# Down-projection of token blocks 0 and 1 as seven block products, with the up-projection's partial sums held in PSUM

## The chip, the core and the metric

The program runs on one core of one Trainium2 chip. TensorE (PE) multiplies, with PEld as its weight loads; VectorE (DVE), ScalarE (ACT) and GpSimd (POOL) do the element-wise work; SyncE (SP) issues most DMAs. The metric is the device time of one execution in microseconds, the median of several runs.

## The reference, cut to what matters

One layer: a combined input projection, chunk-band attention and an mLSTM (together "the mixers"), an output projection, and a feed-forward network with a short convolution. All sums are in float32. The change touches the feed-forward network:

```python
def conv_ffn(h, buf, w_up, w_conv, b_conv, w_down):
    S = h.shape[1]
    u = h @ w_up                                  # 1024 -> 2 * 2816
    ext = jnp.concatenate([buf.astype(u.dtype), u], axis=1)
    y = b_conv
    for j in range(CONV_W):                       # width 3, causal
        y = y + ext[:, j:j + S] * w_conv[j]
    gate, up = jnp.split(y, 2, axis=-1)
    out = (jax.nn.gelu(gate, approximate=True) * up) @ w_down   # 2816 -> 1024
    return out, ext[:, S:]
```

and in the layer: `x = x + rms_norm(conv_ffn(rms_norm(x)))`. There are 2048 prompt tokens (16 tiles of 128) and 8 x 16 sample tokens (one tile).

## The kernel before

Every float32 operand of a matmul is split into a high part (a cast to fp32r, by ACT) and a low part (the rest, by DVE); `mm3` (lines 93 to 97) makes three matmuls of a product: high x high, high x low, low x high. The helper `split` (1264 to 1266) does the two steps for an operand in SBUF, so most splits stand under lines 1265 and 1266 in the profile.

The program has these stages, in order of time:

- **Mixers** (to about 1050 us): 28 weight groups of the input projection (two halves of the tokens, 14 groups each; loop at line 1201). Steps of attention and mLSTM, kept in two pipes, are laid between the projection's steps by `pump` according to planned PE and DVE costs.
- **Output projection** (about 1050 to 1313 us), `project`, which stores the rows x2 in DRAM (`x2d`). `h2_units` prepares the first block's normed, transposed operands.
- **Feed-forward**, three token blocks (`FBLOCKS`: six tiles, six tiles, five tiles), each an up stage and a down stage.

The **up stage** runs over 22 column tiles f of 128 (`NF`), each giving a gate and an up row of 768 tokens. It already uses Winograd's form of Strassen's scheme: seven products P1 to P7 of 4 x 3 matmuls (384 wide, 320 in block 2) in place of eight (`product`, line 1411). The seven token-side operands `B[i]` are made by `h2_units`; the weight-side sums are made in block 0 by four DVE operations per f (`load_quads`, line 1282) and kept in DRAM (`wsd`) for blocks 1 and 2. The products' partial sums x1, x2, x3 are formed in SBUF: one ACT copy (1489) and DVE additions out of PSUM (1491, 1493, 1419, 1508). `conv` then applies the convolution (ACT at 1438, two DVE operations at 1439 and 1440, ACT's gelu at 1442), DVE multiplies gate and up (1514), and the result goes to DRAM (`gd`, 768 values a partition per f).

The **down stage** multiplies that by `w_down` in the plain way: for each half of the output columns `dh`, for each of 22 k, for each of six token tiles one `mm3` of 512 columns (`down`, 1547). The six accumulators are two PSUM banks of tag "mm" and two double banks of tag "big". The operand `gr` is fetched again for each dh and split (`split_g`, 1465) into `gh`, `gl`, held in four buffers of tag "w3", so two k at a time. Weights come four 512-column pieces at a time (`load_down`, 1311) into one of two buffer pairs `wh`, `wl`. Raw fetches land in buffers of tag "q" (`quad`, 512 columns, 11 of them) and "yq" (`row`, 1024 columns, 4 of them). Between the k, `ahead.step()` lays in the next block's `h2_units` and the residual rows of the block before (`later`, 1369: two fetches, a DVE step, a POOL addition, a DMA from POOL's queue).

The tile layer decides the order of the instructions of each engine from the program order, priorities and buffers that come free; it inserts all waits. `keep_in_program_order` pins a DMA's place. Each DMA on SP's queue waits for the one issued eight before it.

## Time and profile before

| | us |
|---|---|
| median of 3 runs (lowest, highest) | 2795.22 (2794.82, 2800.33) |
| span of the profiled execution, first to last instruction | 2784.7 |
| PE busy, DVE busy, ACT busy in that span | 2723.8, 1876.3, 1409.1 |

The page gives a span and no total of the profiled execution; the runs' median is 10.5 us above the span, for what lies before the first and after the last instruction. "Busy" of an engine is the time in which at least one of its instructions ran. Matmuls overlap in the pipeline, so the mean duration of one (about 0.39 us for 512 columns) is longer than the distance between two; what a matmul costs is read as a stretch of time without idle PE divided by the number of matmuls in it. In a table of stretches a row gives the stretch and its length, then busy time and count of PE, PEld, DVE, ACT and POOL, the granted TensorE clock, the DMA engines' busy share and GB/s. In a list of waits a row gives who waited for whom, the total, how often, and the longest. In a list of groups a row ends with the group's busy time and the mean of one in ns, then the engine's idle time before it and who ended it.

### The profile page before, as it was taken

The page shows a single profiled execution, that of the slowest core. Times are in us where ns is not written, and L with a number is a line of the kernel's source. Part 1 is how long each engine was busy: PE and PEld are TensorE (multiplying, and loading weights), DVE is VectorE, ACT ScalarE, POOL GpSimd, SP SyncE. Part 2 cuts the span into 40 slices and gives each one's busy share as a digit, 9 for nine tenths or more (in the row PEclk, how much of TensorE's full clock was granted, in tenths as well). Part 3 has the DMA queues.
Part 4 walks back from the last instruction along what each step waited for, and adds up shares of the span by engine and source line. Part 5 has one row for each costly group of instructions (what it writes and reads, how often), then busy time and mean ns, then how long its engine had stood idle before and what let it go on. Part 6 is the DMA issues. An engine that isn't in the chain of part 4 may idle for free.

```text
span 2784.7 us, 47088 instructions
## 1 busy us (share of the span) xinstructions
PE 2723.8 (98%) x16587; PEld 2548.3 (92%) x16587; DVE 1876.3 (67%) x3447; ACT 1409.1 (51%) x2836; POOL 437.4 (16%) x895
## 2 busy tenths in 40 slices
PE   8999999999999999999999999999999999999998
PEld 7899999998899998888999988899999878999887
DVE  5344455656556668666999986457877864888855
ACT  4355555644356666544454555345455543555543
POOL 1000010212000003244111110011111310222220
PEclk9999999999999999999999999999999999999999
DMA  5544355557555555356655455644544774555585
GB/s 185 155 119 136 103 174 162 164 157 217 162 173 148 144 179 171 107 176 227 187 172 167 167 176 174 219 142 153 160 152 141 276 263 152 172 179 180 192 309 190
DMA packets 311883, 486.05 MB, mean 175 GB/s; under 512 B 55426, under 2 KB 150622, under 8 KB 311518
## 3 DMA queue, kind: packets, MB, share of 16 engines
q1 hardware_dynamic: 271134, 442.92, 50.1%
q10 hardware_dynamic: 38592, 33.83, 3.6%
q0 software_dynamic: 1920, 6.29, 0.6%
q8 instruction: 130, 2.13, 0.3%
q14 instruction: 107, 0.88, 0.1%
HBM read 359.36 MB, written 126.70 MB: 175 GB/s over the span
## 4 chain that ended last, share of the span: by engine, by line
PE 55%; DVE 2%; DMA 1%; issue 1%; ACT 1%; POOL 1%; SPq 0%; DVEq 0%; POOLq 0%; ACTq 0%
PE uec L95 6%; PE uec L96 6%; PE uec L97 6%; PE dn L97 4%; PE dn L96 4%; PE dn L95 4%; PE ua L97 3%; PE ua L95 3%; PE ua L96 3%; PE dnm L97 2%; PE dnm L95 2%; PE dnm L96 2%; PE wo L97 2%; PE wo L95 2%; PE wo L96 2%; PE ub L96 1%
## 5 line engine op out<-in xcount | busy, mean ns | idle before, releaser
L95 PE MATMUL uec<-B,wuh 128*128 128x384 f32 (+1 forms) x720 | 234.9, 328 | 2.2 <-DVE uu L1419 1.1
L96 PE MATMUL uec<-B,wuh 128*128 128x384 f32 (+1 forms) x720 | 235.1, 327 | 0.0
L97 PE MATMUL uec<-B,wul 128*128 128x384 f32 (+1 forms) x720 | 233.9, 327 | 0.0
L1266 DVE TENSOR_TENSOR gl<-gr,gh 128x768 fp32r<-128x768 f32 (+3 forms) x141 | 120.4, 863 | 145.8 <-ACT gh L1265 144.5
L1265 ACT CAST gh<-gr 128x768 fp32r<-128x768 f32 (+3 forms) x141 | 102.0, 735 | 200.1 <-PE dn L96 183.2
L1265 ACT CAST wuh<-wu 128x512 fp32r<-128x512 f32 x255 | 141.7, 617 | 112.1 <-PE uec L96 103.2
L95 PE MATMUL dn<-wdh,gh 128*128 128x512 f32 x466 | 182.4, 391 | 2.3 <-DVE ug L1419 2.3
L96 PE MATMUL dn<-wdl,gh 128*128 128x512 f32 x466 | 183.4, 394 | 0.0
L97 PE MATMUL dn<-wdh,gl 128*128 128x512 f32 x466 | 167.9, 396 | 0.0
L1266 DVE TENSOR_TENSOR wul<-wu,wuh 128x512 fp32r<-128x512 f32 x255 | 164.6, 683 | 2.8 <-DMA x2d<-mx 2.8
L393 DVE CUSTOM_DVE_ANT_0 tmp<-s,nb 128x640 f32<-128x640 f32 (+4 forms) x128 | 94.4, 737 | 96.6 <-PE s L383 94.8
L95 PE MATMUL vo<-wi_h,hT 128*128 128x256 f32 x544 | 155.1, 285 | 0.6 <-DVE mt L199 0.6
L97 PE MATMUL vo<-wi_h,hT 128*128 128x256 f32 x544 | 155.6, 286 | 0.0
L96 PE MATMUL vo<-wi_l,hT 128*128 128x256 f32 x544 | 154.8, 285 | 0.0
L95 PEld LDWEIGHTS uec<-B,wuh 128*128 128x128 f32 x720 | 135.0, 188 | 4.2 <-DVE uu L1419 1.6
L95 PE MATMUL qk<-hT,wi_h 128*128 128x384 f32 (+1 forms) x384 | 128.7, 335 | 7.4 <-ACT qk_st L224 6.6
L96 PEld LDWEIGHTS uec<-B,wuh 128*128 128x128 f32 x720 | 135.2, 188 | 0.2
L97 PEld LDWEIGHTS uec<-B,wul 128*128 128x128 f32 x720 | 135.1, 188 | 0.0
L406 DVE TENSOR_TENSOR ptl<-pt,pth 128x640 fp32r<-128x640 f32 (+4 forms) x128 | 93.6, 737 | 57.1 <-ACT pth L405 56.0
L394 ACT ACTIVATE tmp<-tmp,mn 128x640 f32<-128x640 f32 (+4 forms) x128 | 97.6, 762 | 64.6 <-DVE mn L393 61.9
L96 PE MATMUL qb<-hT,wi_h 128*128 128x384 f32 (+1 forms) x384 | 127.8, 333 | 0.0
L96 PE MATMUL qk<-hT,wi_h 128*128 128x384 f32 (+1 forms) x384 | 127.6, 332 | 0.0
(412 smaller groups left out, 8873.0 us busy)
## 6 DMA issues: line engine op xcount, KB each, us to landing
wu<-in_w_up SPq DMA_DIRECT2D x220, 256.0 KB, 4.1
wu<-wsd SPq DMA_DIRECT2D x176, 256.0 KB, 4.2
wdr<-in_w_down SPq DMA_DIRECT2D x132, 256.0 KB, 5.6
gr<-gd SPq DMA_DIRECT2D x78, 384.0 KB, 3.6
wi_raw<-in_w_in SPq DMA_DIRECT2D x52, 512.0 KB, 4.0
wsd<-ws SPq DMA_DIRECT2D x88, 256.0 KB, 2.8
gd<-g SPq DMA_DIRECT2D x44, 384.0 KB, 3.5
kraw<-kTd SPq DMA_DIRECT2D x112, 128.0 KB, 3.2
```

What stands on the lines that cost most here:

```text
L95: nc.tensor.matmul(out, ah, bh, start=start, stop=False, skip_group_check=onto)
L96: nc.tensor.matmul(out, ah, bl, start=False, stop=False, skip_group_check=onto)
L97: nc.tensor.matmul(out, al, bh, start=False, stop=stop, skip_group_check=onto)
L393: nc.vector.tensor_tensor_reduce(o_, s_, b_, 1.0, 3e38, ALU.add, ALU.min, accum_out=mn)
L394: nc.scalar.activation(tmp[:, :n], tmp[:, :n], AF.Exp, bias=mn, scale=-1.0, accum_out=rsum[:, i % 4, hh:hh + 1])
L406: nc.vector.tensor_tensor(s.ptl[:, sl, qc], ptv, s.pth[:, sl, qc], op=ALU.subtract)
L1265: nc.scalar.copy(h, r)
L1266: nc.vector.tensor_tensor(l, r, h, op=ALU.subtract)
```

## The change

It has five parts.

1. **Seven products in the down stage of blocks 0 and 1** (`FAST`). The activations are cut in four (k below or above 11, first or second three token tiles: A11, A12, A21, A22), the weights likewise (k, output half: B11, B12, B21, B22). `SEQUENCE` names the seven products; each is 11 k x 3 token tiles x `mm3` with 512 columns, and they go alternately into two sets of three PSUM accumulators; every second product of set 0 adds onto what stands there. `leave` copies or adds the sets out after each product. Block 2 keeps the plain form.
2. **The weight differences** T1 to T4 are made once, in the mixers: `folds` fetches w_down in 22 pieces of 512 KB, makes four DVE subtractions of 256 columns on each and stores it to DRAM (`wtd`). A piece is fetched every 12 steps, combined 9 steps and stored 14 steps after its fetch.
3. **The activation sums** S1 to S4 are made in the up stage (`store_a`), four DVE operations of 384 columns for each pair (f, f + 11), in place; they and A11, A12, A22 are stored in DRAM (`ad`) as pieces of 384 columns, seven a pair. f therefore runs in the order 0, 11, 1, 12, ... (`FORDER`).
4. **The up stage's sums in PSUM** in all blocks: P1's result is copied by ACT into bank d, P6 adds onto it, ACT copies d into bank c, P5 and P3 add onto c, P4 adds onto d, P2 onto a. P7 is copied out by ACT. DVE is left with two additions of the up row; the gate row is copied out by ACT. P1 of the next f stands ahead of P4 and P3 of this one. Two pairs of matmuls named "mark" write the double banks once, ahead of block 0.
5. **Buffers**: 12 "q" (11 before), 6 "yq" (4), two `drs` (1); the SBUF scratch of the software DMA queue is set to 4096 bytes a partition; `h2_units` of blocks 1 and 2 is spread over more steps.

```diff
+NK = NF // 2
+FAST = (0, 1)
+FOLD_STEPS = 12
+FORDER = [f for k in range(NK) for f in (k, k + NK)]
...
+            if not late:
+                yield 0.0, 0.0
...
-            for i in range(6):
+            for i in range(6 if late else 8):
...
+    def folds():
...
+        def load(i):
+            k, c = pieces[i]
+            live[i] = v4(pr.tile([P, D], F32, tag="fold", name=f"fold{k}_{c}", bufs=3))
+            tc.keep_in_program_order(nc.sync.dma_start(live[i], v4(I["w_down"][k])[:, :, c * 256:(c + 1) * 256]))
+
+        def combine(i):
+            a, b, c, d = [live[i][:, x] for x in range(4)]
+            for o, x, y in ((a, b, a), (b, c, b), (c, c, a), (d, d, c)):
+                nc.vector.tensor_tensor(o, x, y, op=ALU.subtract)
+
+        def store(i):
+            k, c = pieces[i]
+            tc.keep_in_program_order(nc.sync.dma_start(v4(wtd[k])[:, :, c * 256:(c + 1) * 256], live.pop(i)))
+
+        for n in range(FOLD_STEPS * (len(pieces) + 2)):
+            for lag, do in ((0, load), (9, combine), (14, store)):
+                i, r = divmod(n - lag, FOLD_STEPS)
+                if r == 0 and 0 <= i < len(pieces):
+                    do(i)
+            yield
...
+            if 2 <= gi <= 12:
+                next(fold, None)
...
+    SEQUENCE = [("A11", B11, 0, False), ("A12", B21, 1, False), ("S2", T2, 0, True), ("S4", B22, 1, False),
+                ("S3", T3, 0, True), ("S1", T1, 1, False), ("A22", T4, 0, True)]
...
+        def first(f):
+            a, dc = ps_mm(f"ua{b}_{f}"), ps_big(f"udc{b}_{f}")
+            product(P1, W.pop((P1, f)), a)
+            nc.scalar.copy(dc[:, :n], a[:, :n])
+            return a, dc[:, 0:512], dc[:, 512:1024]
...
-            product(P1, w[0], a)
-            nc.scalar.copy(x1[:, :n], a[:, :n])
-            product(P6, w[1], d_)
-            nc.vector.tensor_tensor(x2[:, :n], x1[:, :n], d_[:, :n], op=ALU.add)
-            product(P7, w[2], e)
-            nc.vector.tensor_tensor(x3[:, :n], x2[:, :n], e[:, :n], op=ALU.add)
-            product(P5, w[3], c)
-            second(uu, x3, c)
...
-            product(P2, w[0], a, onto=True)
-            nc.scalar.copy(ug[:, 2:2 + n], a[:, :n])
-            product(P4, w[1], e, onto=True)
-            nc.vector.tensor_tensor(uu[:, 2:2 + n], x2[:, :n], e[:, :n], op=ALU.add)
-            product(P3, w[2], c, onto=True)
-            second(ug, x2, c)
...
+            product(P6, W.pop((P6, f)), d_, onto=True)
+            nc.scalar.copy(c[:, :n], d_[:, :n])
+            product(P7, W.pop((P7, f)), e)
+            nc.scalar.copy(p7[:, :n], e[:, :n])
+            product(P2, W.pop((P2, f)), a, onto=True)
             nc.scalar.copy(ug[:, 2:2 + n], a[:, :n])
...
+            product(P5, W.pop((P5, f)), c, onto=True)
+            for o, x, y in halves(uu, p7, c):
+                nc.vector.tensor_tensor(o, x, y, op=ALU.add)
...
+                nxt = first(FORDER[fi + 1])
+            product(P4, W.pop((P4, f)), d_, onto=True)
+            nc.vector.tensor_tensor(uu[:, 2:2 + n], p7[:, :n], d_[:, :n], op=ALU.add)
             yu = conv(uu, 1, f)
+            product(P3, W.pop((P3, f)), c, onto=True)
+            for o, _, y in halves(ug, None, c):
+                nc.scalar.copy(o, y)
...
+            def leave(p):
+                acc = sets[SEQUENCE[p][2]]
+                if p in (0, 2, 4, 6):
+                    kept[p] = trio(f"x{p}_")
+                for j in range(3):
+                    if p in (0, 2, 4):
+                        nc.scalar.copy(kept[p][j], acc[j])
+                    elif p == 1:
+                        nc.vector.tensor_tensor(kept[0][j], kept[0][j], acc[j], op=ALU.add)
+                        close(j, 0, kept[0][j])
...
+                    for k in range(4 * c, min(4 * c + 4, NK)):
+                        i = 6 * p + k // 2
+                        if k % 2 == 0:
+                            if i >= 1:
+                                split_a(i + 1)
+                                fetch_a(i + 4)
...
+                        for j in range(3):
+                            tt = slice(k % 2 * 384 + j * P, k % 2 * 384 + (j + 1) * P)
+                            mm3(sets[set_][j], ah[:, tt], al[:, tt], wh[:, wk], wl[:, wk],
+                                start=not onto and k == 0, stop=k == NK - 1, onto=onto)
+                        steps += 1
+                        if steps % 2 == 0:
+                            ahead.step()
+                leave(p)
...
-    nc = bacc.Bacc("TRN2", target_bir_lowering=False, num_devices=1)
+    nc = bacc.Bacc("TRN2", target_bir_lowering=False, num_devices=1, dynamic_dma_scratch_size=4096)
```

In `SEQUENCE` a row is the activation operand, the weight block, the accumulator set and whether the product adds onto what the set holds. `split_a` and `fetch_a` are the activations' `split_g` and `fetch`: one call handles two k of 384 columns, so 768 columns as before, in the same four "w3" buffers; `down_rows` takes the place of the loop in `load_down`, with four 512-column pieces a chunk as before.

## The prediction

> **What bounds the kernel now.** First the page's head and busy times, then a table of eight stretches: the mixers (0 to 1050 us), the output projection (to 1313), and up and down stage of blocks 0, 1 and 2.

> ```profile
> span 2784.7 us, 47088 instructions
> PE 2723.8 (98%) x16587; PEld 2548.3 (92%) x16587; DVE 1876.3 (67%) x3447; ACT 1409.1 (51%) x2836; POOL 437.4 (16%) x895
> ```

> ```profile
> 0.00:1050.00 1050.00, 1014.18 (x7314) 986.44 (x7315) 576.59 (x1410) 547.93 (x1305) 96.91 (x291) 1.00 0.53 159
> 1050.00:1313.00 263.00, 258.01 (x1390) 216.44 (x1389) 186.66 (x290) 126.88 (x302) 96.97 (x130) 1.00 0.49 161
> 1313.00:1642.00 329.00, 322.46 (x1828) 318.80 (x1827) 303.55 (x459) 168.71 (x268) 61.98 (x89) 0.99 0.54 178
> 1642.00:1836.00 194.00, 192.77 (x863) 157.26 (x863) 109.27 (x150) 93.59 (x157) 6.47 (x21) 1.00 0.55 181
> 1836.00:2155.00 319.00, 318.47 (x1828) 318.06 (x1826) 247.04 (x367) 163.96 (x272) 42.99 (x96) 1.00 0.48 154
> 2155.00:2348.00 193.00, 192.39 (x860) 156.00 (x861) 123.70 (x163) 90.63 (x153) 36.99 (x46) 1.00 0.68 230
> 2348.00:2620.00 272.00, 272.00 (x1851) 271.43 (x1850) 235.84 (x480) 155.19 (x274) 64.43 (x182) 1.00 0.56 178
> ```

> PE is idle 1.2 and 0.6 us in the two down stages, 6.5 us in the up stage of block 0, 0.5 in that of block 1, none in that of block 2, at a granted clock of 0.99 to 1.00. So matmuls taken out of a down stage shorten it directly, as long as what feeds PE keeps up. What holds PE up from 1330 us on is this list of waits:

> ```profile
> PE ua L97 <- DVE wul L1266: 3.0, 2, 1.6
> PE dn L95 <- DVE ug L1419: 2.3, 3, 1.4
> PE dnm L95 <- ACT gh L1265: 2.1, 3, 1.5
> PE uec L95 <- DVE uu L1419: 1.1, 1, 1.1
> ```

> with five smaller ones of 3.0 us together: operands that arrive late, none of them for long.

> **What a matmul costs.** Two stretches without idle PE, the first with 512-column matmuls alone, the second with 384-column ones alone:

> ```profile
> 1760.00:1820.00 60.00, 60.00 (x262) 49.02 (x261) 21.84 (x28) 19.23 (x29) 0.00 (x0) 1.00 0.55 180
> 1900.00:2100.00 200.00, 200.00 (x1149) 200.00 (x1148) 156.22 (x231) 101.45 (x164) 25.17 (x55) 1.00 0.47 151
> ```

> 60/262 = 0.229 us and 200/1149 = 0.174 us.

> **Part 1, seven products.** A block's down stage has 22 k x 6 tiles x 2 halves x 3 = 792 matmuls of 512 columns; seven products have 7 x 11 x 3 x 3 = 693. Gone are 198 in two blocks: 198 x 0.229 = 45.3 us. The form of a matmul is the same, and each product's accumulators rest during the product after it (99 x 0.229 = 22.7 us), so no copy out of PSUM should stop PE. The four "mark" matmuls cost 4 x 0.174 = 0.7 us.

> What feeds PE gets more to do in less time (170 us in place of 193). An operand pair of 768 columns still serves 18 matmuls, 4.1 us, but for the same 18 matmuls there are two weight pieces to split in place of one. Rows for it:

> ```profile
> L1266 DVE TENSOR_TENSOR wdl<-wdr,wdh 128x512 fp32r<-128x512 f32 x88 | 58.3, 715 | 9.8 <-ACT wdh L1265 9.8
> L1266 DVE TENSOR_TENSOR gl<-gr,gh 128x768 fp32r<-128x768 f32 x77 | 77.8, 1010 | 107.8 <-ACT gh L1265 107.5
> L1265 ACT CAST wdh<-wdr 128x512 fp32r<-128x512 f32 x88 | 49.3, 617 | 13.9 <-DMA wdr<-in_w_down 7.9 <-PE uec L96 5.9
> L1265 ACT CAST gh<-gr 128x768 fp32r<-128x768 f32 x77 | 64.2, 833 | 132.9 <-PE dn L96 127.6 <-DMA wdr<-in_w_down 3.3 <-DVE f L1376 1.5
> L1340 DVE COPY fr<-dn 128x512 f32<-128x512 f32 x12 | 7.4, 680 | 1.0 <-PE dn L97 1.0
> L1110 ACT COPY b<-h2T_pt 128x512 f32<-128x512 f32 x20 | 11.4, 582 | 3.4 <-PE h2T_pt L1093 2.9 <-PE dn L96 0.5
> ```

> A block has 77 weight pieces (44 before) and 38.5 operand pairs (44). DVE: +33 x 0.715 - 5.5 x 1.010 = +18.0 us; its 12 copies out become 12 additions of about the same 0.68. In block 1: 123.7 + 18.0 = 141.7 of 170 us, 83% (64% before); block 0: 75%. ACT in block 1: 90.6 + 33 x 0.617 - 5.5 x 0.833 + 12 x 0.582 = 113 us, 67%. The row to compare with is the up stage of block 0: DVE is busy 303.6 of 329 us (92%) there and PE idle for 2.0%. So DVE costs between 0 and 2% of 341 us, 6.8. Of the waits at the stages' seams, up to 3 us may go, since the first product needs only one double bank. I take +3 us, bounds -3 to +7.

> The pieces' sizes, from the list of DMA issues (the last column is us from issue to landing):

> ```profile
> wdr<-in_w_down SPq DMA_DIRECT2D x132, 256.0 KB, 5.6
> gr<-gd SPq DMA_DIRECT2D x78, 384.0 KB, 3.6
> ```

> DMA in block 1: 230 GB/s x 193 us = 44.4 MB, + 33 x 0.262 - 5.5 x 0.393 = 50.9 MB, over 170 us 299 GB/s, and the share goes from 0.68 to 0.88. It is uneven even now:

> ```profile
> 2180.00:2200.00 20.00, 20.00 (x96) 16.32 (x95) 19.38 (x23) 12.04 (x19) 9.37 (x10) 1.00 0.96 337
> 2260.00:2280.00 20.00, 20.00 (x89) 16.32 (x88) 10.92 (x15) 10.97 (x21) 1.85 (x6) 1.00 1.01 360
> ```

> The engines were full in both, DVE 97% busy in the first, and PE lost nothing: prefetch carried it. Block 0 comes to 41.6 MB, 244 GB/s. I take no cost; the price without that cover is a rival below.

> **Part 2, weight differences in the mixers.** 22 x 4 DVE subtractions of 256 columns, and 22 fetches and 22 stores of 512 KB. The nearest rows, a 256-column split, and PE's wait for a late fetch in the mixers:

> ```profile
> L356 DVE TENSOR_TENSOR vhl<-vraw,vhl 128x256 fp32r<-128x256 f32 x40 | 16.9, 423 | 18.5 <-ACT vhl L355 18.3
> PE cus L781 <- DMA cs<-in_state_c: 5.0, 6, 2.0
> ```

> 88 x 0.423 = 37 us, against 1050 - 577 = 473 us in which DVE is idle; 23 MB of DMA on 159 x 1050 = 167 MB, a share of 0.60 after 0.53. PE is idle 36 us in the mixers. What is late if this cover fails: a store on SP's queue that waits for its subtraction, or a fetch that waits for a buffer, holds the fetches of attention and mLSTM behind it. A store stands 14 steps behind its fetch. A re-laid order may also save waits. Bounds: -5 (that wait gone) to 22 x 5.0/6 = 18 us. I take +3, 36 us growing like the DMA load (14%, 5 us) being nearer the low end than the high one.

> **Parts 3 and 4, the up stage.** DVE loses three additions of 384 columns per f and gets four subtractions per pair; ACT gets three copies per f more:

> ```profile
> L1493 DVE TENSOR_TENSOR x<-x,uec 128x384 f32<-128x384 f32 x42 | 23.1, 550 | 11.3 <-PE uec L97 11.2
> L1489 ACT COPY x<-ua 128x384 f32<-128x384 f32 x42 | 20.1, 478 | 32.8 <-PE ua L97 32.7
> L1442 ACT ACTIVATE y<-y 128x768 f32<-128x768 f32 x44 | 37.3, 847 | 72.5 <-DVE y L1440 72.5
> ```

> DVE: -3 x 0.55 + 2 x 0.55 = -0.55 us per f in blocks 0 and 1, of about 14.6 us; ACT: +3 x 0.478 = +1.4 us, from 164/319 = 51% to 61% in block 1. New is that PE waits for ACT twice in a chain: P1, copy, P6, copy, P5. In the built program's order 24 to 26 matmuls stand between P6 and P5 of one f (4.2 us) to cover a copy of 0.48. I take 0; low end -6 (the up stages' late operands, 3.0 + 1.1 and smaller ones, vanish); the high end is the third rival. The pieces stored (7 of 192 KB a pair in place of 2 of 384 KB) meet a DMA share of 0.48 to 0.54.

> **Part 5.** Two more bounds by reading: the buffers only relax waits. A smaller scratch may make POOL wait for its previous DMA; nothing that PE needs soon stands behind it but the norm factors of the next block. 0, at most a few us.

> **The sum.** 2784.7 - 45.3 + 0.7 + 3 + 3 + 0 = 2746.1 us of span; the runs' median lies 2795.2 - 2784.7 = 10.5 above it: **2756.6 us**, 1.4% faster. The likeliest case alone: low ends used by half (-8) to -3 + 18 + 7 above, say 2745 to 2778.

> **Rivals.**

> 1. *The mixers' queue is held.* Each of the 22 stores costs PE 0.83 us, the high bound of part 2: 2756.6 - 3 + 18 = 2772. For it: SP issues in order, and PE's waits on DMA exist there. Against: PE's waits from DMAs are few, and the store comes long after its operand. Chance 0.12.
> 2. *The down stage of block 1 becomes DMA-bound.* The extra 6.5 MB fall where the engines are full, at 354 GB/s: +18 us, 2772. For it: the two rows at 0.96 and 1.01. Smaller transfers are slower too: the mixers' 0.53 at 159 GB/s means 300 at a full share, 338 in this stage (230/0.68); at 300 the stage's 50.9 MB take 170 us, exactly its length. Against: those rows show PE not waiting. Chance 0.10. [...]
> 3. *Slower: ACT's copies come late in the up stage.* ACT works in order, and the copy of d into c stands right behind a gelu that waits for the convolution on DVE. Row:

> ```profile
> ACT y L1442 <- DVE y L1440: 93.7, 46, 5.1
> ```

> At its longest, 5.1 + 0.85 + 0.48 = 6.4 us against 4.2 of cover, PE stands 2.25 us; in each of the 44 f of blocks 0 and 1 that is 99 us: 2856. It decides from 0.88 us per f, (2795.2 - 2756.6)/44. For it: DVE is 92% busy in block 0, so its queue is long. Against: the mean of that wait is 93.7/46 = 2.0 us, and it starts before P6 does. Chance 0.09.
> 4. *No gain:* the splits, not PE, set the down stage's pace, and it keeps its 193 us. 2756.6 + 45.3 - 3 = 2799. For it: two weight pieces and an operand pair per 4.1 us through one ACT and one DVE. Against: 83% is below the 92% at which PE lost 2%. Chance 0.05.

> **How the numbers follow.** The forecast has the other 0.64. A difference of 0.2% (5.6 us) is about what a measurement of this kernel can tell from none. Faster: 0.64 + 0.12 + 0.10, less 0.02 for a mild form of rival 3 beside them: 0.84. Same: rival 4 and that mild form, 0.06. Slower: 0.10. The range 2745 to 2788 takes in rivals 1 and 2 and their sum, and leaves out 3 and 4 and little below.

> **What would show it.** Right: 198 fewer 512-column matmuls, stages of about 171 us between the first and last of them in blocks 0 and 1, PE idle below 5 us in each; the output projection starting within 20 us of where it did. Rival 1: longer waits of PE on DMAs before 1050 us. Rival 2: waits of ACT or DVE on wdr or ar fetches in the second down stage, and a share near 1. Rival 3: waits of P5, P6 or P3 on ACT or DVE in every f, and an up stage of block 0 over 340 us. Wrong altogether: PE idle over 45 us more than now.

## The result, and the profile after

The changed kernel takes 2809.85 us (median of 5 runs, 2809.18 to 2815.61); the kernel before, run beside it, 2798.94 (2794.82 to 2800.33). The ratio is 1.0053, with a 95% interval of 1.0038 to 1.0068: slower by 0.5%, where 1.4% faster was forecast. First the head of the page of the profile after, then the table of stretches, cut where the same stages begin in this kernel (mixers and output projection as one, up and down stage of blocks 0, 1 and 2, the tail).

```profile
span 2808.1 us, 47256 instructions
PE 2705.9 (96%) x16393; PEld 2529.3 (90%) x16393; DVE 1888.4 (67%) x3443; ACT 1518.6 (54%) x3164; POOL 451.9 (16%) x895
```

```profile
0.00:1347.00 1347.00, 1286.09 (x8707) 1212.57 (x8708) 788.73 (x1785) 672.55 (x1606) 190.95 (x421) 0.99 0.57 172
1347.00:1691.00 344.00, 328.46 (x1828) 323.40 (x1827) 292.69 (x431) 193.30 (x333) 61.78 (x85) 0.98 0.58 188
1691.00:1865.00 174.00, 170.62 (x766) 138.90 (x765) 129.91 (x190) 112.31 (x201) 18.36 (x30) 1.00 0.72 240
1865.00:2183.00 318.00, 318.00 (x1825) 317.91 (x1824) 236.29 (x338) 188.30 (x333) 42.40 (x90) 1.00 0.57 176
2183.00:2369.00 186.00, 176.22 (x767) 141.04 (x766) 139.46 (x201) 109.92 (x201) 41.67 (x53) 0.97 0.80 272
2369.00:2640.00 271.00, 270.22 (x1839) 269.37 (x1838) 206.45 (x367) 179.97 (x380) 66.19 (x176) 1.00 0.59 181
2640.00:2801.00 161.00, 156.23 (x671) 126.09 (x670) 92.62 (x131) 61.60 (x110) 29.74 (x39) 0.99 0.72 250
```

Against the eight stretches of before: up to block 0's up stage 1313 became 1347 us (+34), that up stage 329 became 344 (+15), down stage 0 194 became 174 (-20), up stage 1 319 became 318 (-1), down stage 1 193 became 186 (-7), up stage 2 272 became 271 (-1), and the rest 165 became 168 (+3). Together +23, the difference of the spans (2808.1 - 2784.7 = 23.4). Part of it is no loss: the profile of before shows a quick execution, as e5 below tells. The matmuls did go: 16587 to 16393 is 194 fewer, 198 less the four marks. So the gain of the down stages is there, in part, and the mixers and up stage 0 ate it.

By kind, PE's idle time rose from 60.9 (2784.7 - 2723.8) to 102.2 us (2808.1 - 2705.9), +41.3. But PE's busy time fell by 17.9 only, not by the 44.6 that the removed matmuls were worth. The mean granted clock says why: 0.998 of full speed before, 0.990 after, so 0.002 x 2784.7 = 5.6 us lost before and 0.010 x 2808.1 = 28 us after. These 22 us are matmuls at half speed; -44.6 + 41.3 + 22 = 18.7 of the 23.4 (the other 5 stay unassigned). The table of stretches of the kernel after, around one stall in up stage 0, shows such a loss:

```profile
1562.61:1566.02 3.41, 3.41 (x21) 3.41 (x21) 2.80 (x5) 1.54 (x2) 0.00 (x0) 1.00 0.54 190
1566.02:1569.44 3.42, 0.76 (x5) 0.44 (x3) 1.38 (x2) 2.55 (x5) 0.00 (x0) 1.00 0.83 159
1569.44:1572.85 3.41, 2.31 (x7) 2.31 (x8) 3.41 (x7) 0.72 (x2) 1.22 (x2) 0.50 0.65 216
1572.85:1576.26 3.41, 3.41 (x12) 3.41 (x12) 2.45 (x5) 1.07 (x2) 1.14 (x2) 0.50 0.61 190
1576.26:1579.68 3.42, 3.42 (x21) 3.42 (x20) 3.11 (x5) 1.64 (x3) 0.49 (x1) 1.00 0.22 83
```

PE stands for 2.66 of 3.42 us. Then the clock is 0.50 for two such windows, and a window without a gap holds 12 matmuls in place of 21. This stall cost its own length and then half of two windows. Of the 13 stretches at a clock of 0.50 in this profile (the end of the program left out) 11 last one window of 3.41 us and two last two.

### The profile page after: what moved, and what is told of

Same layout as the page of the kernel before. It is cut to its first block, busy times and chain, and to the rows that moved or that the text cites. A ratio compares the mean times of both kernels' runs of the same rounds, so it can differ in the third digit from the quotient of the medians.

```text
span 2808.1 us, 47256 instructions
## 1 busy us (share of the span) xinstructions
PE 2705.9 (96%) x16393; PEld 2529.3 (90%) x16393; DVE 1888.4 (67%) x3443; ACT 1518.6 (54%) x3164; POOL 451.9 (16%) x895
## 4 chain that ended last, share of the span: by engine, by line
PE 68%; DMA 14%; DVE 9%; issue 4%; ACT 3%; POOL 1%; SPq 1%; DVEq 0%; ACTq 0%; POOLq 0%
PE udc L101 5%; PE udc L102 5%; PE udc L103 5%; PE dn L103 3%; PE dn L102 3%; PE dn L101 3%; PE ua L102 3%; PE ua L101 3%; PE ua L103 2%; DMA wu<-in_w_up 2%; PE dnm L103 2%; PE pt L73 2%; PE dnm L102 2%; PE dnm L101 2%; PE qb L101 2%
## 5 line engine op out<-in xcount | busy, mean ns | idle before, releaser
L101 PE MATMUL udc<-B,wuh 128*128 128x384 f32 (+1 forms) x720 | 236.6, 329 | 7.0 <-DVE uu L1641 7.0
L102 PE MATMUL udc<-B,wuh 128*128 128x384 f32 (+1 forms) x720 | 235.9, 328 | 0.0
L103 PE MATMUL udc<-B,wul 128*128 128x384 f32 (+1 forms) x720 | 235.6, 328 | 0.0
L101 PEld LDWEIGHTS udc<-B,wuh 128*128 128x128 f32 x720 | 135.9, 189 | 9.1 <-DVE uu L1641 8.9
L1310 DVE TENSOR_TENSOR wdl<-wdr,wdh 128x512 fp32r<-128x512 f32 x198 | 129.1, 699 | 18.6 <-ACT wdh L1309 18.4
L102 PEld LDWEIGHTS udc<-B,wuh 128*128 128x128 f32 x720 | 135.8, 189 | 0.2
L103 PEld LDWEIGHTS udc<-B,wul 128*128 128x128 f32 x720 | 135.7, 189 | 0.0
L1309 ACT CAST wdh<-wdr 128x512 fp32r<-128x512 f32 x198 | 112.7, 617 | 34.9 <-DMA wdr<-in_w_down 10.7
L102 PE MATMUL dn<-wdl,ah 128*128 128x512 f32 x308 | 123.4, 401 | 5.7 <-DVE wdl L1310 5.7
L103 PE MATMUL qk<-hT,wi_l 128*128 128x384 f32 (+1 forms) x384 | 128.0, 333 | 0.0
L103 PE MATMUL qb<-hT,wi_l 128*128 128x384 f32 (+1 forms) x384 | 127.2, 331 | 0.0
## 6 DMA issues: line engine op xcount, KB each, us to landing
wu<-in_w_up SPq DMA_DIRECT2D x220, 256.0 KB, 3.8
wu<-wsd SPq DMA_DIRECT2D x176, 256.0 KB, 4.0
wdr<-in_w_down SPq DMA_DIRECT2D x110, 256.0 KB, 5.3
wsd<-ws SPq DMA_DIRECT2D x88, 256.0 KB, 2.8
wdr<-wtd SPq DMA_DIRECT2D x88, 256.0 KB, 6.3
ar<-ad_S SPq DMA_DIRECT2D x40, 384.0 KB, 4.7
```

Of the source, the lines that this page charges most:

```text
L101: nc.tensor.matmul(out, ah, bh, start=start, stop=False, skip_group_check=onto)
L102: nc.tensor.matmul(out, ah, bl, start=False, stop=False, skip_group_check=onto)
L103: nc.tensor.matmul(out, al, bh, start=False, stop=stop, skip_group_check=onto)
L1309: nc.scalar.copy(h, r)
L1310: nc.vector.tensor_tensor(l, r, h, op=ALU.subtract)
```

## The experiments

Eighteen kernels ran, each against the kernel before on the same chip. Times are medians; the ratio to before has its 95% interval. Beside these runs the kernel before took medians of 2789.36 to 2794.64 us, by the chip, so a time is read through its ratio. "Block 0 starts" is the beginning of its up stage: 1313.5 us in the profile of before, 1347.1 after the change. Rows are from the tables of stretches and have the columns told above, unless a sentence says otherwise.

### Are the weight differences the loss, and what about them?

Eight runs take the folds (the weight differences of part 2) apart. The first leaves them out.

```diff
-    fold = folds()
+    fold = iter(())
-T1, T3, T2, T4 = range(4, 8)
+T1, T3, T2, T4 = range(4)
```

> Leaves the weight differences out: no fetch, subtraction or store in the mixers, and T1 to T4 are plain blocks of w_down; all else as in the changed kernel. Theory A (the folds' steps alone cost the mixers and the output projection their 33.6 us): first matmul of block 0's up stage within 6 us of 1313.5 (changed kernel 1347.1, before 1313.5), time 2776 (2768 to 2784). Theory B (the other edits re-laid the mixers): it starts at 1335 or later and the time stays over 2797.

2778.75 us, 0.9945 [0.9928, 0.9961]; block 0 starts at 1321.5 us. Theory A holds for most: 25.6 of the 33.6 us are the folds'. The other 8.0 belong to the quick execution that was profiled before the change. The matmuls ahead of block 0 stand in the order of before in e1, e3, e5, e10, e14, e16 and e17, and there block 0 starts between 1319.2 and 1327.7 us; with the folds in the mixers it starts between 1339.5 and 1354.4. So single executions scatter by some 8 us, and the loss stands clear of that. Against the full change (1.0053 - 0.9945 = 1.1%) they cost some 30 us, more than one block's seven products can save.

```profile
0.00:1321.00 1321.00, 1278.88 (x8705) 1209.26 (x8706) 761.02 (x1697) 674.01 (x1606) 190.40 (x421) 0.99 0.52 158
```

PE idle is 42.1 us there (1321 - 1278.9), against 60.9 with the folds (1347 - 1286.1). The added idle time is no single wait: PE's waits before block 0 go from 23.3 to 32.9 us on DVE, from 12.1 to 23.4 on ACT, and from 6.0 to 3.3 on DMAs.

Where do the folds wait? Two rows of the changed kernel, the first from DVE's waits before block 0, the second from the list of the instructions on the tile "fold":

```profile
DVE fold L1179 <- DMA fold<-in_w_down: 43.3, 17, 9.4
```

```profile
DMA to landing us min/median/max: 3.8/4.8/7.5
```

The subtractions were asked for nine steps behind their fetch; the tile layer moved them up, and 17 of 22 times DVE stood in front of data that had not landed, 43.3 us in all. Five runs test whether that wait, the subtractions, the queue or the size of the transfers is the cost.

```diff
-            for o, x, y in ((a, b, a), (b, c, b), (c, c, a), (d, d, c)):
-                nc.vector.tensor_tensor(o, x, y, op=ALU.subtract)
+            return
```

> Keeps the 22 fetches and 22 stores of the folds and leaves their 88 DVE subtractions out (w_down is copied as it is). If the cost is DVE standing behind a fetch that has not landed (43.3 us of such waits in the changed kernel): block 0's up stage starts by 1322, time about 2783. If it is the transfers (SP's queue, DMA load): it starts at 1335 or later, time 2797 or more.

2796.6 us, 1.0010 [1.0001, 1.0020]; block 0 starts at 1339.5, idle 54.6 us. By its start that is the second answer: 18.0 of the 25.6 us stay without any subtraction, and so without DVE's wait. The other 6 of the 19 us of extra idle time may be the subtractions' or the scatter of executions.

```diff
-            for lag, do in ((0, load), (9, combine), (14, store)):
+            for lag, do in ((0, load), (22, combine), (28, store)):
```

> The subtractions are asked for 22 steps behind their fetch in place of 9, the stores 28 in place of 14. If the DVE wait on the fetch is the cause and the later place holds in DVE's order: those waits fall from 43.3 us below 10, block 0's up stage starts by 1325, time 2784 to 2790. If the tile layer moves them forward all the same, or the load is the cause: over 1335 and 2800 or more.

2812.1 us, 1.0060 [1.0045, 1.0075]; block 0 starts at 1352.3, and DVE's waits on the fetches are 47.7 us, not below 10. Asking for the subtractions later in the program did not take DVE out of these waits.

```diff
-                nc.vector.tensor_tensor(o, x, y, op=ALU.subtract)
+                nc.gpsimd.tensor_tensor(o, x, y, op=ALU.subtract)
...
-            for lag, do in ((0, load), (9, combine), (14, store)):
+            for lag, do in ((0, load), (14, combine), (24, store)):
```

> The changed kernel with the folds' 88 subtractions on GpSimd in place of VectorE, asked for 14 steps behind the fetch, stores 24. If their place in DVE's order is what spoils the mixers (DVE stood 43.3 us before them): PE idle before block 0 falls from 60.9 to 54 us or less, as without subtractions, and that block starts by 1340. If the transfers and the new order of the mixers are: idle stays at 58 or more, 1345 or later. If GpSimd, standing before a late fetch, holds the mLSTM's mask step behind it: over 1355.

2810.75 us, 1.0058 [1.0043, 1.0074]; block 0 starts at 1349.4. Now GpSimd stands before the fetches (244.3 us) and DVE not at all, and PE is idle 62.7 us. So the loss does not need DVE's 43.3 us of standing still, large as the row is; whether GpSimd's waits took their place is not shown.

The queue and the size were each tried together with an edit of a later stage. In the first, the folds' transfers go through ACT's queue (and the activation sums are made one pair later, which the next part takes up):

```diff
-            tc.keep_in_program_order(nc.sync.dma_start(live[i], v4(I["w_down"][k])[:, :, c * 256:(c + 1) * 256]))
+            tc.keep_in_program_order(nc.scalar.dma_start(live[i], v4(I["w_down"][k])[:, :, c * 256:(c + 1) * 256]))
...
+            held[f] = gt
+            if k == NK - 1:
+                sums_a(k - 1)
+                sums_a(k)
+            elif k:
+                sums_a(k - 1)
```

> The changed kernel with two edits in different stages. (1) The activation sums of a pair are made one pair later, when the stores of its pieces have landed. If DVE's wait for these stores costs up stage 0 its time: that stage goes from 343.6 to 331-334 us, with no DVE wait on a store of ad. If the sums' work itself does: over 339. (2) The folds' fetches and stores go through ACT's queue. If SP's queue is what the transfers hold up: block 0's up stage starts by 1335 (1347.1 in the changed kernel, 1321.5 without folds); if it is the bytes: 1340 to 1350. Time 2785 to 2792 with both, 2798 to 2803 with the first alone.

2816.16 us, 1.0075 [1.0050, 1.0101]; block 0 starts at 1354.4, up stage 0 takes 346 us. Neither edit helps. DVE's waits for the stores of ad stay at 5.1 and 3.1 us: the tile layer put the sums back, and in the trace they stand at the same places of DVE's order as in the changed kernel.

In the second, the folds move in 11 pieces of 1 MiB (and the residual rows leave down stage 1):

```diff
-        pieces = [(k, c) for k in range(NK) for c in range(2)]
+        pieces = [(k, 0) for k in range(NK)]
...
+        done = []
+        if b != 1:
+            done = [u for t, rs in unfinished for u in later(t, rs)]
+            unfinished = []
```

> The changed kernel with two edits in different stages. (1) The residual rows of block 0 are made in block 2's down stage in place of block 1's (24 fetches, 12 stores and 12 DVE steps of 256 KB and 512 columns leave that stage). If DMA and DVE load there cost it 10 us (rival 2): down stage 1 goes from 186.2 to 176 or less, PE idle under 4 us; if its idle time comes from the order of the weight splits: it stays over 182. (2) Folds in 11 pieces of 1 MiB with rows of 2 KB, in place of 22 of 512 KB with rows of 1 KB. If the number or the short rows of the transfers cost the mixers: block 0's up stage starts by 1337; if the bytes do: 1343 or later. Time 2785 to 2800.

2802.32 us, 1.0030 [1.0018, 1.0042]; block 0 starts at 1348.1, idle 61.4 us. DVE's wait on the fetches halves (22.2 us) and nothing else changes. Its second edit did work, see below.

What is left is the bytes, or the order that the tile layer gives everything else once the folds are there. The order of the matmuls ahead of block 0 can be compared in the built programs: without folds it is that of before up to the marks, place by place; with the folds 3617 of 8334 places differ (the expectations below count 7626 places). Two runs are meant to part the two. One moves the bytes and all but leaves the order:

```diff
+            if r == 0 and i < len(pieces):
+                k, c = pieces[i]
+                nc.gpsimd.dma_start(v4(wtd[k])[:, :, c * 256:(c + 1) * 256], v4(I["w_down"][k])[:, :, c * 256:(c + 1) * 256])
+            yield
+            continue
```

> The changed kernel with the folds' bytes and without their place in the order: 22 copies of 512 KB from w_down to wtd inside DRAM, issued by GpSimd (no buffer, no subtraction), T1 to T4 taken as plain blocks of w_down. The order of the mixers' matmuls is that of the kernel without folds but for 112 places of 7626. If the bytes on the DMA engines cost the mixers: PE idle before block 0 52 us or more, that block starts at 1335 or later, time 2790 or more. If the new order does: idle 42 to 46 us, start 1320 to 1328, time 2776 to 2784.

2814.89 us, 1.0085 [1.0070, 1.0100]; block 0 starts at 1354.6. By the letter that is the answer "bytes", but the run was not what it was meant to be. First the copies (count, duration in ns, first and last start in us), then PE's longest wait:

```profile
L1189 POOL DMA_DIRECT2D wtd<-in_w_down x22: 626/626/837, 1.6 to 42.3; - x22
```

```profile
PE hT_pt L73 <- DVE xr L228: 45.7, 5, 40.2
```

With nothing to wait for, all 22 copies were issued in the first 42 us, and the first rows of x came behind them. That wait is 9.8 us in the changed kernel and 11.5 without folds. Less these 34 us, idle time before block 0 is 76.8 - 34.2 = 42.6 us, that without folds. It does not test bytes spread over the mixers.

The other keeps the folds' instructions and moves 8 columns in place of 256:

```diff
-            tc.keep_in_program_order(nc.sync.dma_start(live[i], v4(I["w_down"][k])[:, :, c * 256:(c + 1) * 256]))
+            tc.keep_in_program_order(nc.sync.dma_start(live[i][:, :, 0:8], v4(I["w_down"][k])[:, :, 0:8]))
...
-            a, b, c, d = [live[i][:, x] for x in range(4)]
+            a, b, c, d = [live[i][:, x, 0:8] for x in range(4)]
...
-            tc.keep_in_program_order(nc.sync.dma_start(v4(wtd[k])[:, :, c * 256:(c + 1) * 256], live.pop(i)))
+            tc.keep_in_program_order(nc.sync.dma_start(v4(wtd[k])[:, :, 0:8], live.pop(i)[:, :, 0:8]))
```

> The changed kernel with the folds' order and without their bytes: fetch, subtractions and store as they are, each on 8 columns a row in place of 256 (1/32 of the bytes), T1 to T4 taken as plain blocks. 2880 of the mixers' 7626 matmuls stand at another place than without folds. If the new order costs the mixers: PE idle before block 0 52 us or more, start 1335 or later, time 2790 or more. If the bytes and DVE's 37 us do: idle 42 to 46 us, start by 1328, time 2776 to 2784.

2798.46 us, 1.0037 [1.0025, 1.0050]; block 0 starts at 1344.6.

```profile
0.00:1345.00 1345.00, 1289.42 (x8710) 1213.62 (x8711) 769.58 (x1785) 673.10 (x1606) 188.87 (x421) 0.99 0.51 156
```

Idle is 55.6 us at 156 GB/s, less than the 158 without folds: 23.1 of the 25.6 us come back with 1/32 of the bytes. So the loss does not need the bytes. But this run does not show the order alone: DVE still stands 48.9 us, 18 times, before the small fetches. e2 had 18.0 of the 25.6 us without DVE's waits but with the bytes, and e8 all of them, with GpSimd waiting in DVE's place. What every run with the loss shares is a re-laid order and the transfers' instructions in a queue. That the order is the cause is the reading that fits all of them; no run has a new order without the folds' instructions, so it is argued and not shown. That the same 22 pieces in another order might be free is not excluded either; six orders with the folds' subtractions (this one, the change, and the change with another lag, engine, queue or piece) all start block 0 between 1344.6 and 1354.4 us.

### The scratch and the spread of before

```diff
-    nc = bacc.Bacc("TRN2", target_bir_lowering=False, num_devices=1)
+    nc = bacc.Bacc("TRN2", target_bir_lowering=False, num_devices=1, dynamic_dma_scratch_size=4096)
```

> The kernel before with the smaller DMA scratch alone (4096 bytes a partition); the order of its instructions is the same. If the scratch costs nothing and the profile of before was a quick execution: time within 4 us of before's median, mixers anywhere from 1046 to 1060 with PE idle 36 to 44 us there. If the scratch holds POOL up: 2805 or more, mixers over 1057.

2795.16 us, 1.0007 [0.9996, 1.0018]: no cost. Its profile is a second look at the order of before, and a slower one: span 2793.5 against 2784.7, mixers 1055.9 against 1045.8. Its run took 2795.16 us, 1.7 above the span, and so does every run that shows both (2809.85 and 2808.1 after the change). So the execution that was profiled before the change took 2786.4, not the 2795.2 of the median. Against e5's execution the change loses 14.6 us of span and not 23.4, and block 0 starts 24.1 us later (1347.1 against 1323.0) and not 33.6.

### The up stage: sums in PSUM, activation sums

```diff
-FAST = (0, 1)
+FAST = ()
-    fold = folds()
+    fold = iter(())
```

> Plain down stage in all blocks, no folds, no activation sums: parts 4 and 5 alone. If up stage 0 lost its 15 us to DVE waiting for the stores of the activation pieces (8.3 us of such waits): that stage is back at 328 to 333 us. If it lost them to the copies between the PSUM sums: 340 or more. Down stages 194 and 193 as before. Time 2790 to 2800 by the first with mixers as before, 2805 or more by the second.

2811.58 us, 1.0055 [1.0038, 1.0072]: parts 4 and 5 alone are slower than before. Up stage 0 is 331 us, as the first theory has it, but the total is the second's. The plain down stages have become longer:

```profile
1328.00:1659.00 331.00, 324.75 (x1837) 321.74 (x1837) 276.96 (x396) 195.08 (x336) 61.01 (x88) 0.99 0.53 178
1659.00:1857.00 198.00, 192.05 (x848) 155.82 (x847) 107.75 (x147) 91.05 (x153) 8.20 (x21) 0.99 0.55 177
```

PE is idle 6.0 us in down stage 0, against 1.2 before. Every stage from up 0 to up 2 is 3 to 5 us longer than in e5's profile. No run took this further apart: what parts 4 and 5 cost beside the plain down stages, 0.55% in all, stays open.

```diff
+            x1, x2, x3 = [p4.tile([P, 384], F32, tag="x", name=f"x{i}_{nm}", bufs=3) for i in range(3)]
...
-            nc.scalar.copy(dc[:, :n], a[:, :n])
+            nc.scalar.copy(x1[:, :n], a[:, :n])
...
+            nc.vector.tensor_tensor(x2[:, :n], x1[:, :n], d_[:, :n], op=ALU.add)
```

> The changed kernel with the up-projection's sums made as before (in SBUF by DVE), all else of the change kept, and block 0's residual rows in block 2's down stage. If part 4 is neutral, as my sum had it: up 0 within 4 us of 343.6, up 1 within 4 of 317.8, time as e7_defer_bigfold (2802) within 6. If the PSUM form saves what the activation sums cost DVE: up 0 over 350 and PE idle there over 20. If the PSUM form is what cost the 15 us: up 0 below 335.

2801.7 us, 1.0023 [1.0013, 1.0033], e7's time: up stage 0 takes 341.4 us with the sums in SBUF (344 in PSUM), up 1 320.1 (317.8), up 2 267.6 (270.3). Beside the seven products part 4 is neutral. What up stage 0 loses beyond e3 belongs to part 3, the activation sums and their stores. DVE's waits in that stage, before and then after, and at the end PE's longest row of waits there after the change, on DVE's addition to the up row:

```profile
DVE ws L1282 <- DMA wu<-in_w_up: 12.4, 13, 3.8
```

```profile
DVE ws L1338 <- DMA wu<-in_w_up: 21.2, 16, 3.0
DVE g L1594 <- DMA ad_A<-g: 5.1, 2, 2.6
DVE g L1592 <- DMA ad_A<-g: 3.2, 3, 1.5
PE udc L101 <- DVE uu L1641: 6.2, 5, 3.8
```

Three runs tried it: sums in tiles of their own (with 11 raw buffers, one buffer less for P7's copy and the residual rows moved), stores through GpSimd's queue (with the residual rows in up stage 1), and no sums.

```diff
-            nc.vector.tensor_tensor(a11, a11, a21, op=ALU.subtract)
+            s3_, s2_, s4_ = [p4.tile([P, 384], F32, tag="s", name=f"s{i}_{b}_{k}", bufs=3) for i in (3, 2, 4)]
+            nc.vector.tensor_tensor(s3_, a11, a21, op=ALU.subtract)
```

> The changed kernel with three of the four activation sums of a pair written to tiles of their own in place of over the stored pieces (11 raw buffers in place of 12, two for P7's copy), and block 0's residual rows made in block 2's down stage. If DVE's wait for the stores is what holds up stage 0: no DVE wait on a store of ad there, stage 331 to 335 us in place of 343.6. If DVE's work on the sums (22 us) is: 339 or more. Down stage 1 at 175 again. Time 2788 to 2800.

2815.26 us, 1.0072 [1.0056, 1.0087]. The waits on the stores are gone and the stage is longer, 349.1 us. With one raw buffer less, DVE waits 41.6 us for weights, so the run tells nothing of those waits by themselves:

```profile
DVE ws L1338 <- DMA wu<-in_w_up: 41.6, 19, 3.7
```

```diff
-            put = lambda what, k, src: nc.sync.dma_start(ad[b, what][:, k, :], src)
+            put = lambda what, k, src: nc.gpsimd.dma_start(ad[b, what][:, k, :], src)
...
+        rest = Pipe(iter([u for t, rs in unfinished for u in later(t, rs)] if b == 1 else []))
+            if fi:
+                rest.step()
```

> The changed kernel with the stores of the activation pieces on GpSimd's DMA queue in place of SP's, and block 0's residual rows in block 1's up stage. If SP's queue (stores that wait for DVE, weight fetches behind them) costs up 0 its 12 us: that stage is 335 or less and DVE's waits for weight fetches fall from 21 to under 15 us. If DVE's work or its waits for the stores do: 340 or more. Down stage 1 under 177, up 1 under 321.

2820.77 us, 1.0109 [1.0092, 1.0126]; up stage 0 stays at 341, with 24.8 us of waits for weights. SP's queue is not it. Up stage 1 became 345 us: its cover is worth nothing to the residual rows and the stores on GpSimd.

```diff
-            nc.vector.tensor_tensor(a11, a11, a21, op=ALU.subtract)
-            nc.vector.tensor_tensor(a21, a21, a22, op=ALU.add)
-            nc.vector.tensor_tensor(a22, a22, a11, op=ALU.subtract)
-            nc.vector.tensor_tensor(a12, a12, a22, op=ALU.subtract)
```

> The changed kernel without the four DVE operations that make a pair's activation sums; the same pieces are stored unsummed, so the products take unsummed activations. If DVE's 22 us of sums (and its waits for the stores, which only they have) cost up 0 its 12 us: that stage 329 to 334 us, time about 2798. If the seven stores and 17 MB of a stage do: 339 or more, 2806 or more.

2804.98 us, 1.0039 [1.0025, 1.0053]; the stage is 337 us with 11.8 us idle. That lies between both expectations, and e13, with the sums, has 335.8 and 11.2. So the 15 us of up stage 0 are settled only so far: 5 to 6 us of idle time come with part 3 even without its sums (11.8 against 6.2 in e3), and half clock takes 6.8 us of the stage after the change (half of 13.65 us at a clock of 0.50) against 1.7 before (half of 3.41). The rest is open.

### Down stage 1: bytes, or bunching?

The kernel after, where down stage 1 loses its time and where it does not:

```profile
2210.00:2225.00 15.00, 15.00 (x70) 12.21 (x69) 11.45 (x18) 9.23 (x17) 4.17 (x5) 1.00 1.05 401
2240.00:2255.00 15.00, 11.72 (x43) 9.35 (x43) 11.09 (x15) 7.02 (x16) 6.34 (x9) 0.77 0.99 356
2315.00:2330.00 15.00, 15.00 (x67) 12.19 (x65) 7.16 (x12) 8.35 (x16) 0.00 (x0) 1.00 0.43 125
```

The DMA engines are full both where PE waits and where it does not. PE's longest wait in this stage is 3.3 us on a split of a weight piece, until 2243.3. DVE's timeline just before:

```profile
2237.53 1.27 DVE L1096 SCALAR_TENSOR_TENSOR x2r<-x2r,n_rs,g 128x1024 f32<-128x1024 f32 x1
2238.73 1.27 DVE L1713 TENSOR_TENSOR x<-x,dn 128x512 f32<-128x512 f32 x2
...
2240.52 0.95 DVE L1310 TENSOR_TENSOR al<-ar,ah 128x768 fp32r<-128x768 f32 x1
2241.39 0.68 DVE L1143 TENSOR_TENSOR t<-h2T_pt,t 128x512 f32<-128x512 f32 x1
...
2242.59 1.89 DVE L1310 TENSOR_TENSOR wdl<-wdr,wdh 128x512 fp32r<-128x512 f32 x3
```

The split (wdl) stands behind the next block's norm, the three additions of `leave` and an h2 step, all at once; the residual rows (line 1447) come in the same stretch. In e7 these rows are made in block 2's down stage:

```profile
2181.00:2356.00 175.00, 172.81 (x769) 139.10 (x768) 125.69 (x190) 109.81 (x202) 19.07 (x30) 1.00 0.71 237
2627.00:2791.00 164.00, 158.38 (x671) 126.94 (x670) 105.20 (x143) 61.82 (x110) 53.86 (x63) 0.98 0.84 303
```

Down stage 1 is 174.8 us, 11.4 shorter, and block 2's 3 longer. Whether bytes or bunching was lifted, e17 below tells.

### Both moved to where PE has cover

Four kernels look for places where the change would pay. All use seven products in block 1 alone and the up stage of before, so the mixers keep the order of before.

```diff
-FAST = (0, 1)
+FAST = (1,)
...
+            if b == 1:
+                fold_in(fi)
...
+                fold_out(fi - 1)
```

> Seven products in block 1 alone; the weight differences are made in its up stage (PE idle 0 there, DVE 74% busy) in place of the mixers, one piece of 512 KB an f; up-projection in the form of before; block 0's residual rows in block 2's down stage. If the mixers' tight order, not the differences themselves, is what the folds cost: mixers, output projection, up 0 and down 0 as before (block 1's up stage from 1836 to 1846), up 1 up to 322, down 1 174 to 177: 2772 to 2780, faster than both kernels. If the 37 us of subtractions and 23 MB cost PE wherever they stand: up 1 over 332, 2785 or more.

2806.92 us, 1.0038 [1.0024, 1.0051]. Block 0 starts at 1321.9, as without folds. But up stage 1, with no idle time before, now has 8.5 us and takes 330.8; DVE stands 19.4 us before the pieces. The same hope, the same failure as in the mixers, at half the price; so the folds cost PE time in another stage too. Down stage 1 takes 180 us, and block 2's pays 6 to 8 for the residual rows.

```diff
+                    if b == 0:
+                        fold_step = NF * dh + k
+                        if fold_step % 2 == 0:
+                            fold_in(fold_step // 2)
+                        else:
+                            fold_out(fold_step // 2 - 1)
...
+            if fi:
+                rest.step()
```

> Seven products in block 1 alone; weight differences made in block 0's down stage (PE waits 1.3 us there, DVE 56% busy), block 0's residual rows in block 1's up stage, up-projection as before, and the order 0, 11, 1, 12 in block 1 alone. Mixers to up 0 have the instructions of before. If both new places have room: down 0 195 to 198, up 1 319 to 322, down 1 175 to 177, the rest as before: 2774 to 2780, faster than both kernels. If the differences cost there what they cost elsewhere (12 to 25 us): 2788 or more.

2876.61 us, 1.0304 [1.0286, 1.0323], the slowest. Down stage 0 takes the folds at 198 us, and up stage 1 falls apart under the residual rows:

```profile
1848.00:2263.00 415.00, 340.21 (x1829) 329.76 (x1827) 280.00 (x420) 169.98 (x273) 62.17 (x120) 0.92 0.47 157
```

PE waits 74.8 us, most of it (39.7 and 19.6) for ACT's casts of weights, at a mean clock of 0.92, so 33 us more go to half clock. PE, DVE and ACT are busy for a smaller share than before (DVE 67% against 77%): things wait for each other, not for an engine. SP's queue stands 192.5 us, up to 28.4 at once, before the stores of the activation pieces, which wait for DVE's product of gate and up; that this holds the weight fetches behind them is argued.

```diff
-            if fi:
-                rest.step()
...
+        done = []
+        if b != 1:
+            done = [u for t, rs in unfinished for u in later(t, rs)]
+            unfinished = []
```

> As e14_folds_in_down0, but block 0's residual rows in block 2's down stage, where block 1's own are. If up 1's 414 us came from the residual rows alone: up 1 319 to 321, down 1 174 to 177, down 2 164 to 168, time 2783 to 2789, some 8 us faster than before. If the folds in down 0 reach into up 1: up 1 over 325 and no gain.

2796.15 us, 1.0006 [0.9997, 1.0016]: up stage 1 is back at 321 us, down stage 1 is 174, but down 0 (201), up 0 (333) and down 2 (167) give it all back.

```diff
-                yield (None if i in (0, 3) else next(between, None)) or bubble()
+                yield (next(between, None) if i in ((1, 4, 7) if wide else (1, 2, 4, 5)) else None) or bubble()
...
-        done = []
-        if b != 1:
-            done = [u for t, rs in unfinished for u in later(t, rs)]
-            unfinished = []
+        done = [u for t, rs in unfinished for u in later(t, rs)]
+        unfinished = []
```

> As e16_down0_defer, but block 0's residual rows stay in block 1's down stage, three in place of four to a pair of h2 steps so that they reach further into the stage. If down 1 lost its 10 us to their bunching in its first two thirds (DMA share 1.0 there, 0.4 to 0.6 after): down 1 176 to 180, down 2 160 to 162, time 2780 to 2786. If any place in a seven-product stage is too full: down 1 184 or more, 2788 to 2794.

2790.74 us, 0.9989 [0.9979, 0.9998]: the fastest kernel with the folds in it, within the 0.2% that can't be told from no change. Its down stage 1 answers the question above:

```profile
2178.00:2351.00 173.00, 171.98 (x767) 138.43 (x767) 138.84 (x201) 108.00 (x197) 46.98 (x52) 1.00 0.85 291
```

All residual rows are in it, DVE has the work of the 186-us stage, the DMA engines move more per us (291 against 272 GB/s), and PE waits 1.0 us. The edit puts three steps of the residual rows beside a pair of h2 steps, where the changed kernel's loop has places for six. It was bunching, not bytes. (The folds' place and the form of the up stage differ from the changed kernel too, but neither lies in this stage.)

## Why the prediction was wrong, point by point

- **Seven products save 22.6 us a block: right.** 198 fewer matmuls; with the feeding in order a down stage takes 173 to 175 us (174.6 in block 0, 174.8 and 173.1 in e7 and e17). The 0.229 us of a matmul held: 40.00 us without idle PE (1800 to 1840 us after the change) hold 174 of them, 0.230 each.
- **Down stages "+3 us, bounds -3 to +7" (both blocks together): wrong, by block 1.** Beside the 22.6 us saved, the stages came to +3 in block 0 and +15 in block 1. The load was right: DVE is busy for 139.5 us there, 141.7 in the sum. The sum divided it by the stage's length (83%) and found room. The work comes in bunches at the ends of products, beside norms and residual rows, and the split that PE needs stands behind them in DVE's timeline. With the rows spread (e17) the 11 us are gone.
- **Rival 2 named the place and not the cause.** It asked for 18 us from full DMA engines; down stage 1 lost 11.4, and e17 has the higher rate without the loss. Scaled to a full share, as an estimate, the engines' rate there is 340 GB/s after the change (272/0.80) and 338 before (230/0.68), not the 300 of the mixers (159/0.53); that the size of the transfers makes that difference was not shown. The waits on wdr that it foretold were 4.5 us of ACT, in five pieces, 4.7 before the change.
- **Mixers "+3 us, bounds -5 to 18": the step that failed most.** Up to block 0, with the output projection, which the sum did not charge at all, the folds cost 25.6 us (e1), and 33.6 against the quick profile of before. The term weighed the folds' load (bytes, 37 us of DVE) and used a re-laid order only as a chance of gain. The runs show that load is not the price: 23.1 us stay with 1/32 of the bytes (e13), 18.0 without the subtractions (e2). The folds' instructions and the order that comes with them are what is left; which of the two costs the time stays open.
- **Rival 1 (SP's queue held by stores): not it.** The folds on another queue (e6) cost as much, and PE's waits on DMAs did not grow: on cs 5.0 us before, 3.3 after.
- **Up stages "0": wrong by 13 us, all in block 0.** Rival 3 did not come: the stage did pass the 340 us that it named, but PE waited 0.9 us on the copy into c, and e11 shows part 4 neutral beside the seven products. The term gave part 3 no cost; with it, even without its sums, PE's idle time goes from 6.2 to 11.8 us (e3, e18). Why is open; DVE's waits for weights grow from 12.4 to 21.2 us.
- **Rival 4 (the splits set the pace): no,** since a down stage of 174 us ran.
- **The clock: not in the sum.** Stretches of before are at 0.99 to 1.00, so every stall was priced at its length. 22 us of the miss are half clock.
- **The 10.5 us between span and median** were read as work outside the span. That is 1.7; the other 8.8 were a quick execution. This error went the other way and made the forecast, 53.3 us off in time, look better than its span, 62.0 off (2808.1 against 2746.1).
- **Small slips of the sums:** 2756.6 - 8 is 2748.6 where the range begins at 2745, the rival 2 sum of 2772 leaves out the +3 us that it replaces without saying so, and same and slower should read 0.07 and 0.09. None bears on the miss.

## What to carry to other kernels

Where a planner lays out a tight stage, do not price a new group of instructions by its load alone: here 1/32 of the bytes cost nearly as much as all of them. Compare the built order, and measure the kernel once with the group left out. A stage's mean load says nothing about bunches; look at DVE's timeline where products end. And a stall of PE was not priced by its length alone here: after each of the ten windows of 3.41 us with 2.0 us or more of idle PE in the profile after the change, the next window ran at a clock of 0.50.

## What the runs showed of the hardware

| idle PE in a window of 3.41 us | windows | next window at a clock of 0.50 |
|---|---|---|
| below 1.5 us | 1581 | 0 |
| 1.5 to 1.75 | 8 | 1 |
| 1.75 to 2.0 | 4 | 3 |
| 2.0 and more | 11 | 11 |

So in these two profiles no window at full clock with less than 1.5 us of idle PE had one at half clock behind it, and each of the 11 with 2.0 us or more cost half of the next window too. How a gap lay to the grid counted: before the change PE waits 3.24 us for ACT until 83.03 us, with 1.42 and 1.82 us of it in two windows (border at 81.21 us), and the clock stays at 1.00; after the change the 2.66 us of idle time from 1566.02 to 1569.44 us lie in one window, and the next runs at 0.50. The kernel before ran at mean clocks from 0.994 to 0.999 and in 2784 to 2800 us; that gaps which fall now across a border and now within a window make this difference fits, but was not shown.
